# Loads of a ReLU-and-sum kernel issued by GpSimd, each asked for as one packet, after a first block in three loads from SP

## The chip, the core and the metric

The kernel runs on one core of a Trainium2 chip. The metric is the device time of one execution in microseconds (us), as a median over runs. A profiled execution also gives a span, from the first to the last instruction, some 1.3 us shorter than the device time. The engines have short names: SP (SyncE) only issues loads and stores here, ACT (ScalarE) and DVE (VectorE) compute, and POOL is GpSimd. 16 DMA engines move the data. A "piece" is what one of them moves at a time by the packet records of the trace, which list each transfer with its queue, size, start and duration: a load of 16 rows is 8 pieces of 64 KB on each of them.

## The reference, cut to what matters

```python
x = randn(32, 512, 1024)  # fp32
out = sum(maximum(x, 0), axis=-1)          # [32, 512] fp32
```

There are 16,384 rows of 1,024 numbers: 67.1 MB to read, 64 KB to write. The kernel puts 128 rows of each partition in line, so "a row" below means one row on all 128 partitions, 0.52 MB.

## The kernel before

SP issues every load. Block 0 (16 rows) comes as 1 and 15 rows, six more blocks as one load of 16 rows each, and the last 16 rows in loads of 8, 4 and 2 rows and four pieces of the last two rows. Three buffers of 16 rows turn round: block 3 may load when DVE has summed block 0. In the first six blocks ACT applies the ReLU in place to several rows at a time and DVE sums them (all but four rows of block 5); in block 6 and the tail both engines do whole rows alone. The "seam" is a small buffer for the middle one of the last four pieces.

```python
CHUNKS = [[(0, 0, 1), (1, 0, 15)]] + [[(1, 16 * c + 15, 16)] for c in range(6)]
ACT_STEPS = [[16], [7, 9], [7, 9], [7, 9], [4, 5, 7], [3, 4, 5]]
DVE_STEPS = [[4, 5, 7], [7, 4, 5], [7, 4, 5], [7, 4, 5], [4, 5, 7], [3, 4, 5]]
# ... allocation, semaphores
    for c in range(NBIG + 1):
        if c >= NB:
            sp.wait_ge(s_dve, done[c - NB])          # the buffer is free
        if c < NBIG:
            i = 0
            for g, j, n in CHUNKS[c]:
                sp.dma_start(
                    out=buf[:, c % NB, i : i + n, :], in_=xv[g][:, j : j + n, :]
                ).then_inc(s_in[c], 16)
                i += n
                # ... block 0's issues are moved ahead of the start barrier
# ... the tail's loads from sp in the same way
    for c in range(NTWO):
        alone = BIG - sum(ACT_STEPS[c])
        act.wait_ge(s_in[c], 16 * len(CHUNKS[c]))
        # ... ACT: relu in steps of ACT_STEPS[c], then_inc(s_act, 1)
        # ... DVE: wait s_act, tensor_reduce in steps of DVE_STEPS[c], then_inc(s_dve, 1)
# ... block 6, tail
    act.wait_ge(s_seam, 16 + 2)                      # the seam's load and two partial sums
    act.wait_ge(s_half, 2)
    on_act(seam[:, 0:k], res[:, J - 2 : J - 1]).then_inc(s_last, 1)
    dve.wait_ge(s_seam, 16 + 2)
    on_dve(seam[:, k : k + HEAD + 2], res[:, J - 1 : J]).then_inc(s_last, 1)
```

## Time and profile before

| | kernel before |
|---|---|
| device time, median | 160.95 us (160.78 to 161.04, 3 runs) |
| busy: DVE, ACT, GpSimd | 76%, 64%, 0% of the span |
| block 0 complete | 21.59 us after the span's start |
| step from block to block | 19.35 us |
| last load complete | 157.0 us |

The timeline columns are: start, duration, engine, line, operation, output and input shapes, count, and in brackets how long the engine had been idle and what ended it. Where ACT was idle for a load, its start dates the landing of that load. The lines are shown in the prediction.

### The profile page before, as it was taken

What the parts mean: (1) busy time and instruction counts of PE and PEld (TensorE: products, weight loads), DVE (VectorE), ACT (ScalarE), POOL (GpSimd) and SP (SyncE); (2) the same over time, 40 slices, a digit from 0 to 9 for tenths busy, and PEclk for the clock granted to TensorE, in tenths of its full rate; (3) what the DMA queues carried; (4) which work ended last, traced back from release to release, by engine and by line L of the source; (5) the groups of instructions that cost most, each with busy time, mean ns of one, the idle gap of its engine ahead of it and who ended that gap; (6) DMA issues with size and microseconds to landing.
All of it is one profiled execution on the core that took longest, in us unless ns stands there. A gap on an engine that the chain in (4) does not pass through costs nothing.

```text
span 159.4 us, 150 instructions
## 1 busy us (share of the span) xinstructions
DVE 120.6 (76%) x59; ACT 101.5 (64%) x54; POOL 0.2 (0%) x4
## 2 busy tenths in 40 slices
DVE  0000000009999999999999999999999999898995
ACT  3000059980799708996099941999329980496975
POOL 0000000000000000000000000000000000000000
DMA  9997996996996997989979969969969979798994
GB/s 378 493 401 339 493 526 263 526 526 263 526 493 296 526 444 345 526 378 411 526 312 477 526 263 526 526 263 526 526 263 526 444 345 526 321 469 374 417 400 142
DMA packets 2457, 67.18 MB, mean 421 GB/s; under 512 B 536, under 2 KB 792, under 8 KB 1176
## 3 DMA queue, kind: packets, MB, share of 16 engines
q1 hardware_dynamic: 2456, 67.18, 98.1%
q14 instruction: 1, 0.01, 0.0%
HBM read 67.11 MB, written 0.07 MB: 421 GB/s over the span
## 4 chain that ended last, share of the span: by engine, by line
DVE 55%; DMA 34%; ACT 9%; SPq 2%; issue 0%
DVE res L160 54%; DMA buf<-in_x_dram 34%; ACT buf L145 9%; SPq L101 1%; SPq L112 1%; DVE buf L130 0%; DVE seam L130 0%; SPq L91 0%; DVE turned L169 0%
## 5 line engine op out<-in xcount | busy, mean ns | idle before, releaser
L160 DVE TENSOR_REDUCE res<-buf 128x4 f32<-128x4096 f32 (+3 forms) x18 | 99.4, 5596 | 35.5 <-ACT buf L145 35.5
L145 ACT ACTIVATE buf<-buf 128x7168 f32<-128x7168 f32 (+5 forms) x13 | 80.4, 6233 | 46.1 <-DMA buf<-in_x_dram 46.1
L127 ACT ACTIVATE buf<-buf 128x1024 f32<-128x1024 f32 (+2 forms) x19 | 19.0, 999 | 8.9 <-DMA buf<-in_x_dram 8.9
L130 DVE TENSOR_SCALAR_CACHE_REDUCE buf<-buf 128x1024 f32<-128x1024 f32 (+2 forms) x19 | 20.7, 1143 | 1.7 <-DMA buf<-in_x_dram 1.6
L127 ACT ACTIVATION_READ_ACCUMULATOR buf<-buf 128x1 f32 x19 | 3.6, 188 | 0.0
L145 ACT ACT_TABLE_LOAD x1 | 1.3, 1283 | 1.3 <-PEq L223 1.3
L130 DVE DVE_READ_ACCUMULATOR buf<-buf 128x1 f32 x19 | 1.6, 84 | 0.0
L130 DVE TENSOR_SCALAR_CACHE_REDUCE seam<-seam 128x258 f32<-128x258 f32 x1 | 0.4, 421 | 0.0
L127 ACT ACTIVATE seam<-seam 128x114 f32<-128x114 f32 x1 | 0.3, 300 | 0.1
L169 DVE STREAM_TRANSPOSE turned<-res 128x32 f32<-128x32 f32 x1 | 0.2, 211 | 0.0
L127 ACT ACTIVATION_READ_ACCUMULATOR seam<-seam 128x1 f32 x1 | 0.2, 186 | 0.0
L223 POOL MEMSET const-bfloat16-1.0<- 128x1 bf16 x1 | 0.1, 101 | 0.0
L223 POOL MEMSET const-uint8-127<- 128x1 uint8 x1 | 0.1, 101 | 0.0
L223 POOL MEMSET const-float32-0.0<- 128x1 f32 x1 | 0.1, 98 | 0.2 <-issue 0.2
L223 POOL MEMSET const-float32-1.0<- 128x1 f32 x1 | 0.1, 98 | 0.0
L130 DVE DVE_READ_ACCUMULATOR seam<-seam 128x1 f32 x1 | 0.1, 82 | 0.0
## 6 DMA issues: line engine op xcount, KB each, us to landing
buf<-in_x_dram SPq DMA_DIRECT2D x1, 7680.0 KB, 21.1
buf<-in_x_dram SPq DMA_DIRECT2D x1, 4096.0 KB, 25.3
buf<-in_x_dram SPq DMA_DIRECT2D x1, 2048.0 KB, 29.9
buf<-in_x_dram SPq DMA_DIRECT2D x1, 1024.0 KB, 31.9
buf<-in_x_dram SPq DMA_DIRECT2D x1, 512.0 KB, 3.3
buf<-in_x_dram SPq DMA_DIRECT2D x1, 456.0 KB, 32.5
buf<-in_x_dram SPq DMA_DIRECT2D x1, 256.0 KB, 32.7
seam<-in_x_dram SPq DMA_DIRECT2D x1, 184.0 KB, 32.6
```

Of the source, the lines that this page charges most:

```text
L101: sp.dma_start(out=buf[:, tb, r : r + n, :], in_=xv[-1][:, r : r + n, :]).then_inc(s_in[NBIG + i], 16)
L112: sp.dma_start(out=flat[:, lo:hi], in_=rows[:, lo:hi]).then_inc(s_in[NBIG + len(TAIL) + k], 16)
L127: return act.activation(t, t, AF.Relu, accum_out=acc)
L130: return dve.tensor_scalar(out=t, in0=t, scalar1=0.0, scalar2=None, op0=ALU.max, op1=ALU.add, accum_out=acc)
L145: act.activation(t, t, AF.Relu).then_inc(s_act, 1)
L160: dve.tensor_reduce(out=res[:, c * BIG + r : c * BIG + r + n], in_=buf[:, c % NB, r : r + n, :], axis=X, op=ALU.add,).then_inc(s_dve, 1)
L169: dve.transpose(out=turned[:, :], in_=res[:, 0:32]).then_inc(s_turn, 1)
L223: nc = _bacc.Bacc("TRN2", target_bir_lowering=False, num_devices=1)
```

## The change

Its intent: give the stream of loads fewer and larger packets, issue it from the idle GpSimd, and hide the start of GpSimd's first load behind the last 3 rows of block 0, while ACT and DVE begin on the first 13.

```diff
-CHUNKS = [[(0, 0, 1), (1, 0, 15)]] + [[(1, 16 * c + 15, 16)] for c in range(6)]
-ACT_STEPS = [[16], [7, 9], [7, 9], [7, 9], [4, 5, 7], [3, 4, 5]]
-DVE_STEPS = [[4, 5, 7], [7, 4, 5], [7, 4, 5], [7, 4, 5], [4, 5, 7], [3, 4, 5]]
+CHUNKS = [[(0, 0, 1), (1, 0, 12), (1, 12, 3)]] + [[(1, 16 * c + 15, 16)] for c in range(6)]
+ACT_STEPS = [[13, 3], [7, 9], [7, 9], [7, 9], [7, 9], [3, 4, 5]]
+DVE_STEPS = [[4, 9, 3], [7, 4, 5], [7, 4, 5], [7, 4, 5], [7, 4, 5], [3, 4, 5]]
 ...
+    i = 0
+    for g, j, n in CHUNKS[0]:
+        sp.dma_start(out=buf[:, 0, i : i + n, :], in_=xv[g][:, j : j + n, :]).then_inc(
+            s_in[0] if i + n < BIG else s_rest, 16
+        )
 ...
+    pool.wait_ge(s_in[0], 16 * 2)
+    for c in range(1, NBIG + 1):
         if c >= NB:
-            sp.wait_ge(s_dve, done[c - NB])
+            pool.wait_ge(s_dve, done[c - NB])
 ...
+            pool.dma_start(
+                out=buf[:, c % NB, :, :], in_=xv[g][:, j : j + n, :], single_packet=True
+            ).then_inc(s_in[c], 16)
 ...   (the tail's seven loads likewise: pool, single_packet=True)
+            if c == 0 and r == 13:
+                act.wait_ge(s_rest, 16)
 ...
-    act.wait_ge(s_seam, 16 + 2)
+    act.wait_ge(s_end, 16)
+    act.wait_ge(s_seam, 2)
     act.wait_ge(s_half, 2)
 ...   (DVE likewise)
```

More of the change, by code (lines that the diff above doesn't have):

```diff
@@ L58, in bass_relu_sum_kernel @@
     s_in = [nc.alloc_semaphore(f"s_in{i}") for i in range(n_in)]
+    s_rest = nc.alloc_semaphore("s_rest")
     s_act = nc.alloc_semaphore("s_act")
@@ L64, in bass_relu_sum_kernel @@
     s_seam = nc.alloc_semaphore("s_seam")
+    s_end = nc.alloc_semaphore("s_end")
     s_last = nc.alloc_semaphore("s_last")
@@ L68, in bass_relu_sum_kernel @@
     s_out = nc.alloc_semaphore("s_out")
-    sp, act, dve = nc.sync, nc.scalar, nc.vector
+    sp, act, dve, pool = nc.sync, nc.scalar, nc.vector, nc.gpsimd
     NTWO = len(ACT_STEPS)
@@ L84, in bass_relu_sum_kernel @@
     )
-    for c in range(NBIG + 1):
+    i = 0
[3 more added lines that the diff above has]
+        )
+        i += n
+        code.insert(arrival, code.pop())
+        arrival += 1
+    pool.wait_ge(s_in[0], 16 * 2)
+    for c in range(1, NBIG + 1):
         if c >= NB:
-            sp.wait_ge(s_dve, done[c - NB])
+            pool.wait_ge(s_dve, done[c - NB])
         if c < NBIG:
-            i = 0
-            for g, j, n in CHUNKS[c]:
-                sp.dma_start(
-                    out=buf[:, c % NB, i : i + n, :], in_=xv[g][:, j : j + n, :]
-                ).then_inc(s_in[c], 16)
-                i += n
-                if c == 0:
-                    code.insert(arrival, code.pop())
-                    arrival += 1
+            [(g, j, n)] = CHUNKS[c]
+            pool.dma_start(
+                out=buf[:, c % NB, :, :], in_=xv[g][:, j : j + n, :], single_packet=True
+            ).then_inc(s_in[c], 16)
     r = 0
@@ L100, in bass_relu_sum_kernel @@
     for i, n in enumerate(TAIL):
-        sp.dma_start(out=buf[:, tb, r : r + n, :], in_=xv[-1][:, r : r + n, :]).then_inc(
-            s_in[NBIG + i], 16
-        )
+        pool.dma_start(
+            out=buf[:, tb, r : r + n, :], in_=xv[-1][:, r : r + n, :], single_packet=True
+        ).then_inc(s_in[NBIG + i], 16)
         tail.append((r, n, s_in[NBIG + i]))
@@ L111, in bass_relu_sum_kernel @@
     for k, (lo, hi) in enumerate((first, second, third)):
-        sp.dma_start(out=flat[:, lo:hi], in_=rows[:, lo:hi]).then_inc(
+        pool.dma_start(out=flat[:, lo:hi], in_=rows[:, lo:hi], single_packet=True).then_inc(
             s_in[NBIG + len(TAIL) + k], 16
         )
-    sp.dma_start(out=seam[:, 2 : 2 + w + HEAD], in_=rows[:, CUT : D + HEAD]).then_inc(s_seam, 16)
+    pool.dma_start(
+        out=seam[:, 2 : 2 + w + HEAD], in_=rows[:, CUT : D + HEAD], single_packet=True
+    ).then_inc(s_end, 16)
     sp.wait_ge(s_turn, 1)
@@ L139, in bass_relu_sum_kernel @@
         alone = BIG - sum(ACT_STEPS[c])
-        act.wait_ge(s_in[c], 16 * len(CHUNKS[c]))
+        act.wait_ge(s_in[c], 16 * (1 if c else 2))
         r = 0
@@ L151, in bass_relu_sum_kernel @@
         if alone:
-            dve.wait_ge(s_in[c], 16 * len(CHUNKS[c]))
+            dve.wait_ge(s_in[c], 16)
             for i in range(BIG - alone, BIG - alone // 2):
@@ L173, in bass_relu_sum_kernel @@
     for c in range(NTWO, NBIG):
-        act.wait_ge(s_in[c], 16 * len(CHUNKS[c]))
-        dve.wait_ge(s_in[c], 16 * len(CHUNKS[c]))
+        act.wait_ge(s_in[c], 16)
+        dve.wait_ge(s_in[c], 16)
         for i in range(BIG):
@@ L198, in bass_relu_sum_kernel @@
     on_dve(flat[:, lo:hi], seam[:, k + HEAD + 1 : k + HEAD + 2]).then_inc(s_seam, 1)
-    act.wait_ge(s_seam, 16 + 2)
+    act.wait_ge(s_end, 16)
+    act.wait_ge(s_seam, 2)
     act.wait_ge(s_half, 2)
     on_act(seam[:, 0:k], res[:, J - 2 : J - 1]).then_inc(s_last, 1)
-    dve.wait_ge(s_seam, 16 + 2)
+    dve.wait_ge(s_end, 16)
+    dve.wait_ge(s_seam, 2)
     on_dve(seam[:, k : k + HEAD + 2], res[:, J - 1 : J]).then_inc(s_last, 1)
```

## The prediction

> **What bounds the kernel now.** I read the page first, then the timeline, then the chain of waits in order of time, then the waits of the SP queue. The page of the kernel before:
>
> ```profile
> span 159.4 us, 150 instructions
> DVE 120.6 (76%) x59; ACT 101.5 (64%) x54; POOL 0.2 (0%) x4
> q1 hardware_dynamic: 2456, 67.18, 98.1%
> HBM read 67.11 MB, written 0.07 MB: 421 GB/s over the span
> ```
>
> No compute engine is near its limit (76% and 64% of the span), while the one queue that carries all loads keeps the 16 DMA engines busy for 98.1% of it. A share is only an average, so the next question is whether any stage runs at another pace. The timeline gives the pace: the ACT engine sits idle until a load is there, so the start of its first instruction on each block is the moment of landing.
>
> ```profile
> 21.61 13.86 ACT L145 ACTIVATE buf<-buf 128x16384 f32<-128x16384 f32 x1 [19.06 <-DMA buf<-in_x_dram]
> 40.97 13.95 ACT L145 ACTIVATE buf<-buf 128x7168 f32<-128x7168 f32 x2 [5.50 <-DMA buf<-in_x_dram]
> 60.31 13.95 ACT L145 ACTIVATE buf<-buf 128x7168 f32<-128x7168 f32 x2 [5.39 <-DMA buf<-in_x_dram]
> 79.67 13.95 ACT L145 ACTIVATE buf<-buf 128x7168 f32<-128x7168 f32 x2 [5.41 <-DMA buf<-in_x_dram]
> ...
> 118.36 10.63 ACT L145 ACTIVATE buf<-buf 128x3072 f32<-128x3072 f32 x3 [5.31 <-DMA buf<-in_x_dram]
> ```
>
> The reader is to see equal steps: 40.97, 60.31 and 79.67 are 19.34 and 19.36 us apart, and from 40.97 to 118.36 four blocks took 77.39 us, 19.35 each. A block is 16 rows of 4 KB on 128 partitions, 8.39 MB, so the loads run at 8.39 / 19.35 = 433.5 GB/s without a pause, whatever DVE and ACT do. One row is 1.21 us. The whole run is then 8 blocks x 19.35 = 154.8 us, plus 21.61 - 19.35 = 2.3 us before the stream is at its pace, which makes 157.1; the last load lands at 157.0 in the chain of waits:
>
> ```profile
> 0.45 21.14 DMA buf<-in_x_dram
> 21.61 13.87 ACT buf L145
> 35.50 34.59 DVE res L160 x6
> ...
> 124.39 32.60 DMA buf<-in_x_dram
> ...
> 157.01 0.44 DVE buf L130 x2
> 157.47 0.43 DVE seam L130 x2
> ```
>
> This chain is a trap. It gives 54% of the span to DVE, because the last loads were issued when DVE gave a buffer back (at 122.05). But that load took 32.6 us from issue to landing, though its data need far less: it stood in line behind block 6, which landed only at 137.72. Issued some 13 us later, it would still have landed at the same time. So I take the stream of loads, and not DVE, as the bound. The SP queue's own waits say the same from the other side:
>
> ```profile
> SPq L91 <- DVE res L160: 101.6, 4, 50.7
> SPq L101 <- DVE res L160: 16.9, 1, 16.9
> ```
>
> The first long wait ends at about 52 us (block 0 is given back), while block 2 is still arriving until 60.3. There are some 8 us of stock in the queue at the tightest place, so these waits leave no hole, as the equal steps show.
>
> [...] The trace before has no GpSimd load; for SP its packet records show 1.0 us from the first issue to the first packet. [...]
>
> **The change part by part.**
>
> *Packets.* In the packet records before, a piece of 65,536 B took 2.418 us (median) on its engine and one of 32,768 B 1.213 us. The difference, 1.205 us per 32,768 B, is the pure data rate: 27.2 GB/s an engine, 435 GB/s for 16. Twice 1.205 is 2.410, so each packet carries about 8 ns on top. An engine handles 8 packets of each load. After the change 13 loads come from GpSimd (6 blocks, 3 of the tail, 4 of the last two rows): 104 pieces in 13 packets, 91 boundaries fewer. At 8 ns that is 0.7 us, all of it on the path, because the stream is the path. Whether the 8 ns belong to the packet or to the piece I can't see; I take 0.5 us.
>
> *The hand-over.* GpSimd waits for 13 rows, then issues block 1, while 3 rows (3 x 1.21 = 3.6 us) are still in flight. The delay from the semaphore to the first GpSimd packet is hidden if it is below 3.6 us less the delay of the semaphore behind the data (0.3 us between a load's last packet and its last semaphore count in the records), some 3.3 us. [...] Expected cost: 0 to 0.5 us, I take 0.1.
>
> *Issue.* SP loses issues of 0.33 to 0.5 us each, GpSimd gets them[...]. Both lie beside the stream: the tightest re-issue has some 8 us of stock. Cost 0.
>
> *The split of block 0.* ACT starts at 13 rows, near 21.6 - 3.6 = 18.0 us instead of 21.61, and gives DVE 13 rows after 13/16 of 13.86 us, at about 29.3 instead of 35.50: DVE starts 6 us sooner. It gains nothing at the end, since DVE then waits for block 1 at 41, plus 6.2 us of ACT. It only makes the stock larger: block 0 is given back at about 46 (29.3 plus 16 rows at some 1.07 us a row) instead of 52. The new steps of block 4 make no difference to the end either: at 99.0 us, ACT's 7 rows take 6.2, DVE's 16 rows about 17.3, so it is given back near 122.5, as before at 122.05.
>
> *The tail.* Same pieces, same work; 157.0 to the end stays at 2.4 us.
>
> Sum: 160.95 - 0.5 + 0.1 = 160.5 us.
>
> **The rivals.** (a) *The three rows get stuck.* [...] (b) *A hole at the hand-over*: if the first GpSimd load needs 5 us, the stream stands still for nearly 2 us, 162 to 162.5. [...] (c) *GpSimd's loads run slower*, by 1 or 2%[...]: 162 to 163.5. [...] (d) *The change frees DVE and the whole gets much faster*: the chain's 54% speaks for it, the equal steps of 19.35 against it; the page's DMA share leaves under 2%.
>
> **Range and chances.** The gain can't well exceed 0.7 us of packets plus a little: 159.9 is the low end. Upward (b) and a mild (c) reach 162.2. The 2% marks are 157.7 and 164.2. [...] Slower is mostly (a), with some of (c): 0.09. The rest is 0.89.
>
> **What would show it.** In the timeline after: ACT's first start near 18.0, then blocks landing 19.27 to 19.35 us apart, the shorter if the 8 ns are saved; block 1 at about 41.0 if the hand-over has no hole; the queue part of the page with far fewer packets; GpSimd's waits on DVE ending well before the block in flight lands. Wrong would be: a landing step over 19.4 (c), block 1 later than 41.5 (b), ACT's three rows starting after 30 us (a), or a chain of waits in which an ACT or DVE wait now ends after the stream.

The sum came to 160.95 - 0.5 + 0.1 = 160.5 us. No trace before has a load from GpSimd, so the 0.1 is the author's guess. The 0.5 comes from the packet records, but that each load becomes one packet an engine, and that the 8 ns go with the packet, were assumptions. The working of rival (a) came to 168 to 169 us, and the chance of faster, 0.02; by the trace, DMA engines that are busy for 98.1% of the span leave under 2%.

## The result, and the profile after

The changed kernel takes **161.11 us** (161.03 to 161.18, 4 runs), the kernel before 160.89 us in the same comparison. The ratio is 1.0013 with a 95% interval of 0.9996 to 1.0030: the same time. (A ratio here is the mean time of one kernel's fast runs over that of the other's of the same rounds, so it isn't quite the ratio of the medians.) The interval holds 1; variants below whose intervals do not will nevertheless show the 0.2 us to be there.

The page of the changed kernel: first the span, then the engines' busy time, then the queues with packets, MB and their share of 16 engines' span.

```profile
span 159.7 us, 152 instructions
DVE 121.3 (76%) x59; ACT 101.5 (64%) x54; POOL 7.2 (5%) x17
...
q0 software_dynamic: 1568, 58.72, 85.2%
q1 hardware_dynamic: 728, 8.45, 12.7%
```

The loads have moved to another queue, and the two queues together are busy for 97.9% of the span, as the one was before. The page's number of packets, of which the prediction expected far fewer, doesn't fall to 13 loads: it still records each piece by itself.

The timeline of the changed kernel:

```profile
18.13 13.95 ACT L156 ACTIVATE buf<-buf 128x13312 f32<-128x13312 f32 x2 [15.11 <-DMA buf<-in_x_dram]
18.41 1.20 POOL L102 DMA_DIRECT2D buf<-in_x_dram  x2 [17.97 <-DMA buf<-in_x_dram]
29.46 17.34 DVE L171 TENSOR_REDUCE res<-buf 128x4 f32<-128x4096 f32 x3 [29.46 <-ACT buf L156]
41.17 13.95 ACT L156 ACTIVATE buf<-buf 128x7168 f32<-128x7168 f32 x2 [9.09 <-DMA buf<-in_x_dram]
47.09 0.53 POOL L102 DMA_DIRECT2D buf<-in_x_dram  x1 [27.49 <-DVE res L171]
...
60.52 13.95 ACT L156 ACTIVATE buf<-buf 128x7168 f32<-128x7168 f32 x2 [5.40 <-DMA buf<-in_x_dram]
...
118.58 10.63 ACT L156 ACTIVATE buf<-buf 128x3072 f32<-128x3072 f32 x3 [5.41 <-DMA buf<-in_x_dram]
```

ACT and DVE start earlier as planned (18.13 and 29.46 instead of 21.61 and 35.50), and block 3 is issued at 47.09. Then the same march begins: from 41.17 to 118.58 four blocks take 77.41 us, 19.35 each, where they took 77.39 before. The only difference is an offset: block 1 lands 0.2 us later, and so does every block after it.

The end of the chain of waits of the changed kernel (start, duration, what):

```profile
125.93 31.27 DMA buf<-in_x_dram
157.20 0.02 issue
157.22 0.44 DVE buf L139 x2
157.66 0.03 issue
157.69 0.02 DVEq L215
157.71 0.07 issue
157.78 0.43 DVE seam L139 x2
```

The last load ends at 157.20 instead of 156.99. In the whole chain the share of DVE's sums has fallen from 54% to 12% of the span, and the time hasn't changed. Between the last two DVE groups there are now 0.12 us instead of 0.02: DVE's sequencer (DVEq) passes one wait more.

### The profile page after: what moved, and what is told of

It reads as the page before. It is cut to its first block, busy times and chain, and to the rows that moved or that the text cites. A ratio compares the mean times of both kernels' runs of the same rounds, so it can differ in the third digit from the quotient of the medians.

```text
span 159.7 us, 152 instructions
## 1 busy us (share of the span) xinstructions
DVE 121.3 (76%) x59; ACT 101.5 (64%) x54; POOL 7.2 (5%) x17
## 2 busy tenths in 40 slices
DMA packets 2297, 67.18 MB, mean 421 GB/s; under 512 B 552, under 2 KB 552, under 8 KB 888
## 4 chain that ended last, share of the span: by engine, by line
DMA 66%; ACT 17%; DVE 13%; POOL 2%; issue 1%; SPq 0%; DVEq 0%
DMA buf<-in_x_dram 66%; ACT buf L156 17%; DVE res L171 12%; POOL buf L108 1%; POOL buf L119 1%; DVE buf L139 0%; DVE seam L139 0%; SPq L89 0%; DVEq L215 0%
## 5 line engine op out<-in xcount | busy, mean ns | idle before, releaser
L171 DVE TENSOR_REDUCE res<-buf 128x4 f32<-128x4096 f32 (+4 forms) x18 | 100.1, 5600 | 35.7 <-ACT buf L156 35.7
L102 POOL DMA_DIRECT2D buf<-in_x_dram x6 | 3.3, 552 | 100.7 <-DVE res L171 82.8
L108 POOL DMA_DIRECT2D buf<-in_x_dram x3 | 1.6, 527 | 18.8 <-DVE res L171 18.8
L119 POOL DMA_DIRECT2D buf<-in_x_dram x3 | 1.6, 539 | 0.0
L122 POOL DMA_DIRECT2D seam<-in_x_dram x1 | 0.5, 536 | 0.0
```

What stands on the lines that cost most here:

```text
L102: pool.dma_start(out=buf[:, c % NB, :, :], in_=xv[g][:, j : j + n, :], single_packet=True).then_inc(s_in[c], 16)
L108: pool.dma_start(out=buf[:, tb, r : r + n, :], in_=xv[-1][:, r : r + n, :], single_packet=True).then_inc(s_in[NBIG + i], 16)
L119: pool.dma_start(out=flat[:, lo:hi], in_=rows[:, lo:hi], single_packet=True).then_inc(s_in[NBIG + len(TAIL) + k], 16)
L122: pool.dma_start(out=seam[:, 2 : 2 + w + HEAD], in_=rows[:, CUT : D + HEAD], single_packet=True).then_inc(s_end, 16)
L171: dve.tensor_reduce(out=res[:, c * BIG + r : c * BIG + r + n], in_=buf[:, c % NB, r : r + n, :], axis=X, op=ALU.add,).then_inc(s_dve, 1)
```

## The experiments

The theory was: the stream of loads is the bound before and after; the cost of 8 ns goes with each piece, not with each packet, so the packet part of the change saves nothing; and the hand-over of the stream from SP to GpSimd is just hidden. The rivals: one packet per load does save something that is lost elsewhere; GpSimd's issue costs the 0.2 us; the queues change only at whole packets, and the 3 rows are tuned to avoid that. Twelve kernels were run; all gave correct results.

### All loads from SP again, the split kept

```diff
-    pool.wait_ge(s_in[0], 16 * 2)
-            pool.wait_ge(s_dve, done[c - NB])
+            sp.wait_ge(s_dve, done[c - NB])
-            pool.dma_start(..., single_packet=True)
+            sp.dma_start(...)                      # the tail's loads too
```

> The changed kernel with every load issued by SP again, so that of the change only the split of block 0 (1, 12 and 3 rows) and the new steps of ACT and DVE remain. Theory A (the stream is the bound, and the 0.2 us that the changed kernel lost come from the added piece boundary in block 0): 161.1 us, block 0 complete near 21.8 us after the span's start. Theory B (the 0.2 us belong to GpSimd's issue): 160.9 us, block 0 complete near 21.6. If the earlier start of DVE were worth anything: under 160.5.

Measured: 161.10 us, ratio to before 1.0014 (1.0002 to 1.0027). That is the time of the changed kernel without GpSimd and without the packets. Block 0 is complete at 21.80 us in its records of semaphores, as in the changed kernel, and at 21.59 before. So neither the issuing engine nor the packets have a net effect; what little there is belongs to the rest of the change. DVE's earlier start, which this kernel has too, gains nothing.

### GpSimd's loads without the demand for one packet

```diff
-            pool.dma_start(..., single_packet=True)
+            pool.dma_start(...)                    # all 13 loads
```

> The changed kernel without the demand for one packet per load. Theory A (the 8 ns go with each piece, not with each packet): 161.1 us, blocks 19.35 us apart. The prediction's step (packets cost 8 ns each and one packet had saved them, given back elsewhere): up to 0.7 us more than the changed kernel, 161.6 to 161.8, blocks 19.40 or more apart.

Measured: 161.07 us (160.94 to 161.22), against 161.11 with it. In the timeline ACT starts on blocks 1 and 5 at 41.05 and 118.44, 77.39 us for four blocks, 19.35 each. The packet records have the same sizes in both. The demand for one packet had no visible effect at all. Whether it was obeyed, and the pieces really were joined, no record shows.

### Pieces of 16 KB, from GpSimd and from SP

The six blocks' loads are cut so that one piece moves 16 KB instead of 64 KB (4,601 packets on the page instead of 2,297); from GpSimd still with the demand for one packet per load.

```diff
-            pool.dma_start(..., single_packet=True)
+            pool.dma_start(..., single_packet=True, max_dma_last_dim=16384)
```

> The changed kernel with the six blocks that GpSimd loads cut into pieces of 16 KB, still one packet per load. Before, a 64 KB piece took 2.418 us and a 16 KB piece 0.611, so four of these are 26 ns longer; 48 pieces of 64 KB per engine are cut. Theory A (the cost goes with the piece): 48 x 26 ns = 1.25 us more than the changed kernel, 162.3 us, blocks 19.56 us apart. Rival (it goes with the packet): unchanged, 161.1 us, 19.35 apart.

> The same cut with all loads issued by SP. Theory A: 1.25 us more than the same kernel from SP with whole pieces, about 162.2 to 162.4 us. If the cut costs this much from SP and nothing from GpSimd, one packet per load does save the 8 ns, but only where there are several pieces to a packet that can be merged.

Measured: 162.39 us from GpSimd and 162.42 us from SP, ratios to before 1.0095 and 1.0097. The timeline of the GpSimd version:

```profile
41.42 13.95 ACT L156 ACTIVATE buf<-buf 128x7168 f32<-128x7168 f32 x2 [9.43 <-DMA buf<-in_x_dram]
...
119.75 10.63 ACT L156 ACTIVATE buf<-buf 128x3072 f32<-128x3072 f32 x3 [5.64 <-DMA buf<-in_x_dram]
```

Four blocks took 78.33 us, 19.58 each instead of 19.35. The whole costs 162.39 - 161.11 = 1.28 us, where the theory had said 1.25. From SP it costs 162.42 - 161.10 = 1.32. So the fixed cost goes with the piece whichever engine issues it, and asking for one packet per load does not take it away. This is the step on which the predicted gain rested. Two readings remain: the pieces were joined and the cost stays with each of them, or they weren't joined, so that every piece was still a packet.

### One and two rows in flight at the hand-over

Block 0 comes as 1, 14 and 1 rows, and as 1, 13 and 2; GpSimd waits for the first two loads. For one row:

```diff
-CHUNKS = [[(0, 0, 1), (1, 0, 12), (1, 12, 3)]]
-ACT_STEPS = [[13, 3],      DVE_STEPS = [[4, 9, 3],      if c == 0 and r == 13:
+CHUNKS = [[(0, 0, 1), (1, 0, 14), (1, 14, 1)]]
+ACT_STEPS = [[15, 1],      DVE_STEPS = [[4, 11, 1],     if c == 0 and r == 15:
```

> Block 0 comes as 1, 14 and 1 rows and GpSimd waits for 15 rows, so only 1.2 us of loads are in flight at the hand-over in place of 3.6. Theory A (the delay from the semaphore to GpSimd's first packet is real, up to 2.8 us in the changed kernel's records, and the three rows just hide it): a hole of 1 to 1.9 us, 162.1 to 163.0 us, block 1 landing at 42.1 to 43.0 instead of 41.15. Rival (the delay is under 1 us): 161.1 us, block 1 at 41.2.

> The changed kernel with block 0 as 1, 13 and 2 rows and GpSimd waiting for 14 rows: 2.4 us in flight at the hand-over. With one row left the first GpSimd packet started 1.7 us after the semaphore and took 3.0 to 3.6 us instead of 2.4, and block 1 was 2.4 us late. If the delay is 1.7 us and the rest of the lateness comes from the idle engines: 2 rows (2.1 us after the semaphore) hide nearly all, 161.1 to 161.4 us, block 1 at 41.1 to 41.4. If the lateness falls in proportion to the rows, 1.2 us a row: 162.2 us, block 1 at 42.3.

Measured: 163.28 us with one row (ratio 1.0151), 162.29 us with two (1.0093). The timelines, one row first:

```profile
20.80 1.20 POOL L102 DMA_DIRECT2D buf<-in_x_dram  x2 [20.36 <-DMA buf<-in_x_dram]
...
43.51 6.18 ACT L156 ACTIVATE buf<-buf 128x7168 f32<-128x7168 f32 x1 [9.04 <-DMA buf<-in_x_dram]
```

```profile
19.52 1.20 POOL L102 DMA_DIRECT2D buf<-in_x_dram  x2 [19.09 <-DMA buf<-in_x_dram]
...
42.31 6.18 ACT L156 ACTIVATE buf<-buf 128x7168 f32<-128x7168 f32 x1 [9.11 <-DMA buf<-in_x_dram]
```

Block 1 is late by 43.51 - 41.17 = 2.34 us and by 42.31 - 41.17 = 1.14 us. Each row taken from the stock in flight costs 1.2 us, which is just the time to load a row. My first estimate for two rows, nearly all hidden, was wrong; the proportional one held. Going back from this (1.21 + 2.34 and 2.42 + 1.14 us), some 3.5 us must be in flight, and 3 rows, 3.6 us, leave no hole.

The packet records with one row left say what this consists of. GpSimd's issue starts 0.3 us after the semaphore, and the 16 engines begin their first piece of it 1.4 to 1.9 us after that, at 22.21 to 22.68 us, when they had finished with SP's last pieces at 21.0 to 21.4. The first pieces then took 3.0 to 3.6 us in place of 2.42. With two rows left they began at 20.92 to 21.98, about when SP's pieces ended, and still took 3.1 us on average; with three rows left they took 2.42. Why a first piece that comes late is slow isn't shown. So the rows in flight must hide both the delay to the first piece and its slow start.

### Six rows in flight at the hand-over

```diff
-CHUNKS = [[(0, 0, 1), (1, 0, 12), (1, 12, 3)]]
+CHUNKS = [[(0, 0, 1), (1, 0, 9), (1, 9, 6)]]      # ACT 10 and 6 rows, DVE 4, 6 and 6
```

> Block 0 comes as 1, 9 and 6 rows and GpSimd waits for 10 rows, so that some 4 us of SP's loads are still outstanding when GpSimd's first packet comes. If an engine changes between queues only after a whole packet of 512 KB (19.3 us): several of the 6 rows' pieces are stuck, the six rows land after 55 us, and the kernel takes 166 to 172 us. If it shares piece by piece: the six rows land near 31 us, harmless, 161.1 us.

Measured: 161.11 us, ratio 1.0017. The timeline:

```profile
14.62 1.20 POOL L102 DMA_DIRECT2D buf<-in_x_dram  x2 [14.19 <-DMA buf<-in_x_dram]
...
28.92 5.32 ACT L156 ACTIVATE buf<-buf 128x6144 f32<-128x6144 f32 x1 [5.83 <-DMA buf<-in_x_dram]
...
41.02 6.18 ACT L156 ACTIVATE buf<-buf 128x7168 f32<-128x7168 f32 x1 [6.78 <-DMA buf<-in_x_dram]
```

The six rows land at 28.9 us, not after 55, and block 1 at 41.0 as ever. The packet records show, from 19.0 us on, a 64 KB piece of GpSimd's queue and a 24 KB piece of SP's in turn. That is 4.7 us after the semaphore, while 1.7 us were enough on idle engines, with one row left: the engines first went on with SP's pieces, and why so long stays open. Handing over this early cost nothing (161.11 us): the same bytes moved in another order. Handing over late did cost something: 162.29 us with two rows left, 163.28 us with one.

### No wait at the hand-over, with one packet per load and without

```diff
-    pool.wait_ge(s_in[0], 16 * 2)
```

> The changed kernel without GpSimd's wait for 13 rows, so blocks 1 and 2 compete with block 0 from the start. If an engine changes queues only after a whole packet of 512 KB: one piece of block 0 passes per 19.3 us, block 0 lands near 58 to 60 us, DVE gives it back near 88, and the stream stands still: 185 to 195 us. If it shares piece by piece: block 0 lands near 40 to 45 us, 165 to 176 us. If the queue that came first is served first: 161 us.

> The same without the demand for one packet. If the packet is the unit of change and this is what one packet per load decides: block 0 lands clearly earlier than in the run with one packet, near 40 to 45 us, 165 to 176 us. If packets don't matter for the sharing: the same time as with one packet, within 1 us.

Measured: 173.21 us and 173.10 us (ratios 1.0768 and 1.0761). The DMA view between 17 and 25 us, with one packet per load and then without (packets, MB, share of the 16 engines):

```profile
q0 software_dynamic: 26, 1.70, 49.1%
q1 hardware_dynamic: 32, 1.57, 45.4%
```

```profile
q0 software_dynamic: 26, 1.70, 49.2%
q1 hardware_dynamic: 32, 1.57, 45.5%
```

Both queues move at once, GpSimd's in pieces of 64 KB and SP's in pieces of 48 KB, one for one (in the records such a pair takes 4.23 us), in both kernels alike. So the first 13 rows land only at 35.09 us. Then the last three rows, in pieces of 12 KB, take turns with pieces of 64 KB, one pair in 2.9 us, and land at 58.28 us, after block 1 (38.15). The expectation for sharing by pieces had put block 0 at 40 to 45 us: it overlooked that taking turns piece by piece left the queue of small pieces a small share, 12 KB of every 76 at the end. The loss that follows shows in the timeline of the first:

```profile
35.11 11.30 ACT L155 ACTIVATE buf<-buf 128x13312 f32<-128x13312 f32 x1 [32.08 <-DMA buf<-in_x_dram]
46.44 14.08 DVE L170 TENSOR_REDUCE res<-buf 128x4 f32<-128x4096 f32 x2 [46.44 <-ACT buf L155]
58.31 36.51 ACT L155 ACTIVATE buf<-buf 128x3072 f32<-128x3072 f32 x6 [11.90 <-DMA buf<-in_x_dram]
...
64.75 0.53 POOL L101 DMA_DIRECT2D buf<-in_x_dram  x1 [61.30 <-DVE res L170]
```

ACT begins at 35.11 instead of 18.13 and then stands idle for 11.90 us until the three rows are there; DVE begins at 46.44 instead of 29.46, and GpSimd may issue block 3 only at 64.75, when the three buffers had been full since 60.7. This is the case in which DVE does become the bound: the stream stands still, and DVE never gets its lead back (from 74.94 on, the chain of waits runs through DVE to the end). How much of the 12 us the late 13 rows cost and how much the three, no run separates. So GpSimd's wait is needed here (173.21 us without it), though its exact place isn't: 3 rows and 6 rows left gave the same 161.11 us.

### The small offset, part by part

Three kernels undo the large parts: the kernel before with one small thing of the change each, or more of it.

```diff
 # split_only and split_six: the kernel before, with
-CHUNKS = [[(0, 0, 1), (1, 0, 15)]]
+CHUNKS = [[(0, 0, 1), (1, 0, 12), (1, 12, 3)]]
+CHUNKS = [[(0, 0, 1), (1, 0, 3), (1, 3, 3), (1, 6, 3), (1, 9, 3), (1, 12, 3)]]
 # end_wait_only: the kernel before, with the seam's load on s_end and
-    dve.wait_ge(s_seam, 16 + 2)
+    dve.wait_ge(s_end, 16)
+    dve.wait_ge(s_seam, 2)                         # ACT likewise
```

> The kernel before with one thing of the change: block 0 comes as 1, 12 and 3 rows in place of 1 and 15. Two small causes compete for the 0.2 us that every variant of the changed kernel has lost. Theory C: about half comes from the added load (8 more pieces per engine at 8 ns, 0.06 us, and up to 0.15 us in block 1's landing) and half from the added wait at the end: 160.95 us, block 1 landing 41.0 to 41.15. If the split is all of it: 161.1. If none: 160.85.

> The kernel before with one thing of the change: the seam's load counts on its own semaphore, so ACT and DVE wait once more before their last instruction. In the chain of the changed kernel the time between the last two DVE groups is 0.12 us instead of 0.02. Theory C: 0.1 us more than before, 160.95 us, and the same 0.12 us in the chain. If the end wait costs nothing: 160.85.

> The kernel before with block 0 in six loads (1, 3, 3, 3, 3 and 3 rows) in place of two: four more loads, the cost of a load's boundary four times. By pieces alone: 4 x 8 x 8 ns = 0.26 us, 161.1 us. If each added load costs the 0.2 us that one added load seemed to cost: 0.8 us, 161.7 us.

Measured, with the kernel before at 160.85 us in the same comparison: split_only 161.11 us (ratio 1.0016, interval 1.0004 to 1.0029), end_wait_only 160.88 us (1.0006, 0.9992 to 1.0020), split_six 161.13 us (1.0017, 1.0004 to 1.0029). In the timelines ACT starts on block 0, and on block 1, at

```profile
21.83 13.86 ACT L145 ACTIVATE buf<-buf 128x16384 f32<-128x16384 f32 x1 [18.80 <-DMA buf<-in_x_dram]
...
41.18 13.95 ACT L145 ACTIVATE buf<-buf 128x7168 f32<-128x7168 f32 x2 [5.50 <-DMA buf<-in_x_dram]
```

with three loads, and with six loads at

```profile
21.90 13.86 ACT L145 ACTIVATE buf<-buf 128x16384 f32<-128x16384 f32 x1 [17.22 <-DMA buf<-in_x_dram]
...
41.26 13.95 ACT L145 ACTIVATE buf<-buf 128x7168 f32<-128x7168 f32 x2 [5.50 <-DMA buf<-in_x_dram]
```

The split alone makes the whole offset: 0.26 us in time, 0.22 us in the start on block 0 (21.83 against 21.61). It is not a cost per load, as three more loads (six in place of three) added only 0.07 us to that start, and 0.02 us to the time. The added wait at the end shows in the chain of end_wait_only (0.12 us between the last two DVE groups), but its 0.03 us in time can't be told from none. Theory C, half from each, fell.

What makes the first split cost 0.2 us stays open. Eight more pieces per engine at 8 ns are 0.06 us. In the six-load kernel pieces alone would give 0.26 us, near what was seen there (0.29 us); in the three-load kernels they don't suffice, and single profiles of the variants with three loads put block 0 anywhere between 21.66 and 21.80 us.

No run beat the kernel before, and none pointed to a version that would: the step of 19.35 us is the same in every kernel with 64 KB pieces whose stream doesn't stand still, and each thing that the change adds around the stream costs nothing or a little.

## Why the prediction was right or wrong

**Right in range and class.** 161.11 us lies between 159.9 and 162.2, and within 2% of before. The point, 160.5, was 0.6 us low, and its sign was wrong: a small gain was forecast and a small loss came.

**The bound: right.** The landing step is 19.35 us before and after. Warning of the chain's 54% for DVE was right too: with DVE six microseconds ahead, the last load lands no earlier.

**Packets: the step that failed.** The prediction put "At 8 ns that is 0.7 us, all of it on the path" and took 0.5 us of it, while it left open whether the 8 ns belong to the packet or to the piece. They stay with the piece, whatever is asked of the packet: a 64 KB piece of GpSimd's queue took 2.418 us as one of SP's did, dropping the demand for one packet left 161.07 us, and four times as many pieces cost 1.28 us from GpSimd with that demand and 1.32 us from SP without it. The term of the sum is 0 in place of -0.5. Whether joined pieces keep their cost or were never joined stays open; that asking for one packet saves nothing is shown.

**Hand-over: right in cost, wrong in its working.** The sum took 0.1 us, and the step of block 1 after block 0 (21.80 to 41.15) leaves no hole. But the estimate of the delay to GpSimd's first packet was too short. Measured with one row left, on idle engines, the delay is 1.7 to 2.2 us, and the slow first piece (3.0 to 3.6 us in place of 2.42) has to be hidden as well, so about 3.5 us are needed and 3.6 us were there. That no hole came was thus partly luck. With 2 rows that estimate would have said "no hole"; the run showed 1.1 us.

**Issue: right in cost.** GpSimd takes 0.53 us for an issue in the timeline (1.20 us for the first two together), where SP took 0.33 to 0.5, and block 3 is issued at 47.09 with block 2 landing at 60.5. Block 4 was given back at 123.0 us (122.5 said, 122.05 before); as the last loads stand in line behind block 6 anyway, this cost nothing.

**The split of block 0: right for ACT and DVE, wrong for the stream.** ACT at 18.13 (18.0 said), DVE at 29.46 (29.3 said), and no gain at the end. That the split itself would cost the stream was not considered: 0.2 to 0.26 us, of which the added pieces explain 0.06. This is the second error of the sum: -0.5 becomes 0, the +0.1 for the hand-over becomes 0, and +0.2 is added.

**Tail: nearly right.** The added wait is 0.1 us in the chain and not resolved in the time.

**The rivals.** (a), the stuck rows, did not come, and its working (cut) rested on an assumption that the runs refute: the queues took turns piece by piece, 64 KB and 24 KB with six rows in flight, which cost nothing (161.11 us). A milder form does exist: without the wait the three rows took turns with pieces of 64 KB and landed at 58.28 us. (b), the hole, was seen, at 1.1 us with two rows and 2.3 us with one, but not with three. (c), a slower stream from GpSimd, did not come: 19.35 us a block. (d), DVE as the bound, was wrong for this change, and becomes true only in the run without the wait. An issue by GpSimd took the same time whether DVE was busy or not: 0.54 us at 126.45 while DVE summed, 0.53 us at 65.26 while DVE was idle.

## What to carry to other kernels

Where loads land at equal steps, with the DMA engines busy for 98.1% of the span, changing who issues them or how they are packed gained nothing here (161.11 us against 160.89) and added small edges around the stream; look for a smaller number of bytes, or for the time before and after the stream. When a stream passes from one queue to another, keep enough in flight to cover the delay to the new queue's first packet and its slow first piece (some 3.5 us here), and hand over too early (161.11 us with six rows left) rather than too late (162.29 us with two), but not so early that many small pieces that the first consumer needs must take turns with large ones (173.21 us without the wait). A long bar in the chain of waits is no bound if the load that it released stood in line anyway: here the share of DVE's sums fell from 54% to 12% of the span, and the time stayed (160.89 and 161.11 us).
